# A diffusion-step kernel on one core: lent buffers to the end of their phase, a quiet inverse, and a row normed ahead

## The chip, the cores and the metric

The kernel runs on one core of one Trainium2 chip. The metric is the device time of one execution in microseconds (us), the median over several executions. The engines are called as the profile calls them: PE (TensorE, its matrix multiplications), PEld (its weight loads, which overlap PE), DVE (VectorE), ACT (ScalarE), POOL (GpSimd) and SP (SyncE, which here only issues DMAs). All of them run their own queue in order and wait for each other by semaphores.

## The reference, cut to what matters

One transformer-like layer for 128 context tokens and 128 latent tokens, D = 2048, in float32, weights shared by both:

```
h  = rmsnorm(x, norm1_g) * (1 + scale1) + shift1          # scale, shift, gate: six rows of silu(cond) @ w_mod
(hq, hi, ..., gates) = split(h @ w_in)                    # 17440 columns
o_a = hgrn2(...)          # mixer A, gated linear recurrence, both directions
o_b = chunk_mlp(...)      # mixer B
o_c = rmsnorm(gdn_scan(...), onorm_g) * silu(g_raw)       # mixer C, delta rule with an inverse of I + L
merged = sum(sigmoid(gates_i) * (o_i @ w_br_i))
x = x + gate1 * (merged @ w_out)
x = x + gate2 * (square(relu(h2 @ w_ff1)) @ w_ff2)        # h2 = norm and modulation of x by rows 3 and 4
y = rmsnorm(x, final_g)
```

The outputs are y for both token rows and the final states of mixers A and C for the context. In mixer C the latent row starts from a cached state, the context row from zero.

## The kernel before, in words

**Weights stream past stationary activations.** All 256 tokens stay on chip. Each weight matrix is cut into units of 128 x 1024 floats (512 KB). SP issues one DMA per unit in the order of use. For each unit, ACT rounds it to a high part (`wh`, "CAST wh<-raw") and DVE subtracts to get the low part (`wl`), and PE multiplies three products of high and low parts: 24 matmuls of 256 columns or 12 groups of 512. In the profile `pb` are the banks of these products, `pf` are the banks of all smaller work.

**The start phase.** The first 88 units (`self.lend`) are eight groups of eight units of w_mod for rows 0 and 1 (`in_wmods`, used whole, without a split, by short matmuls "pf<-raw,cst") and, between them, 24 units of w_in (`in_win`, `in_winh`). After each group of eight, a `chain` turns the sums into columns (ACT "COPY m<-pf", PE "pf<-sel,m", DVE "modc", "gs"), and `modulate` makes two columns of the normalised input (DVE "tp", ACT "ACTIVATE tp" and "CAST Hh", DVE "Hl"). The w_in units of a group need the columns of that group.

**Where units land.** There are three load buffers of their own (`raw`). In the start phase, twelve more are lent from six large slots (z3, z4, z5, z6, z7, z0, two halves each) that later hold other things. `run_stream` takes buffers from a list `raws` in first-in order; `issue` loads as long as the list holds one, and a buffer goes back to the list once its unit has been split or used whole. A lent one goes back only while the number of issued units is under `last`; `last = self.lend - len(raws)` is 88 - 15 = 73. Two pairs of high and low parts (slots z8 and z9) are lent in the same way.

**The order of all other work is made by a planner in the program.** `Clock` and `Meter` keep an estimated time for each engine as instructions are written out. Work beside the stream is written as generators (fillers). `pump` lets them go on while DVE and ACT are estimated to be less than a margin ahead of PE. A DMA is estimated to take its bytes divided by 3.6e5 per us, after those before it. Nothing of this estimate runs on the chip: what comes out is one fixed order per engine.

**Modulation sums in the background.** Rows 2 to 5 of w_mod are summed on DVE (`mods`: "junk<-mraw,cb", two sums for each of 128 units `in_wmodr`). `quota(m)` says how many stream units must have gone before unit m of these may be summed: 24 until 30 units after the start phase, 84 until the mark b (which stands ahead of the third branch product `in_wbr`), 96 until 24 units before the end of w_out, the rest in the feed-forward part.

**Mixer C.** `gdn_all` first makes eight blocks and spills them to memory ("sp<-z"), then inverts 32 x 32 diagonal blocks with 31 steps on DVE ("m<-m,m"), then runs `gdn_second` for eight pairs of heads in two chains (slots z3 and z4): four for the latent row (s = 1), then four for the context row. Each reloads a spilled block ("z<-sp"), and those of the latent row also a cached state ("z<-in_s0gd"). Then `norm_gate` norms both rows (`head_rms`), gates them, transposes them and splits them into `och` and `ocl`, which the third branch product needs.

Of the kernel before, what the change touches and what calls it, by code (L numbers as in the profile page):

```python
# [116 lines left out]
class Meter:  # L117
# [34 lines left out]
    def __getattr__(self, name):  # L152
# [3 lines left out]
        def g(*a, **k):  # L156
# [5 lines left out]
            if name == "dma_start":  # L162
# [3 lines left out]
                clock.dma = max(clock.dma, start + DMA0) + size / 3.6e5  # L166
# [30 lines left out]
class Backbone:  # L197
# [173 lines left out]
    def rsqrt(self, v, n, tag, scale=None):  # L371

        nc = self.nc
        r, t = self.small(n, f"rs{tag}"), self.small(n, f"rt{tag}")
# [17 lines left out]
    def run_stream(self, steps):  # L392
# [10 lines left out]
        last = self.lend - len(raws)  # L403
# [366 lines left out]
    def quota(self, m):  # L770

        a, b, c, d, e = self.marks
        for n, lo, hi, n1 in ((0, a, a+30, 24), (24, a+30, b, 84), (84, b, c, 96)):
            if m < n1:
                return lo + (hi - lo) * (m - n) / (n1 - n)
        return d + (e - d) * (m - 96) / 32

    def mods(self, chs):
# [15 lines left out]
        for m, (ch, kq, n) in enumerate(todo):  # L794
# [8 lines left out]
            while not self.forced and self.units < self.quota(m):  # L803
                yield W
# [18 lines left out]
    def head_rms(self, x4):  # L823

        nc = self.nc
        ss = self.small(16, "ss")
        for s in range(2):
            for f in range(2):
                i, t = yield from self.gettmp()
                for h in range(4):  # L830
                    c = 8 * s + 4 * f + h
                    nc.scalar.activation(t[:, h * P:h * P + P], x4[:, s, 4 * f + h, :], AF.Square, accum_out=ss[:, c:c + 1])
# [4 lines left out]
        r = yield from self.rsqrt(ss, 16, "hd")  # L837
        yield W
        for s in range(2):
            for h in range(8):  # L840
                nc.scalar.activation(x4[:, s, h, :], x4[:, s, h, :], AF.Copy, scale=r[:, 8 * s + h:8 * s + h + 1])
                yield 1

    def norm_gate(self, otm, gate, gcol, hi, lo):
# [3 lines left out]
        yield from self.head_rms(otm)  # L848

        def part(j):  # L850
            o = otm[:, :, 2 * j:2 * j + 2, :]
            nc.vector.tensor_tensor(out=o, in0=o, in1=gate[:, :, 256 * j:256 * j + 256].rearrange("p s (h d) -> p s h d", h=2), op=ALU.mult)
# [381 lines left out]
    def gdn_all(self):  # L1234
# [16 lines left out]
        yield 1.2  # L1251
        for j in range(31):
# [5 lines left out]
            yield 0.15 + 2.1e-3 * n * w  # L1258
        nc.vector.transpose(self.AD.rearrange("p m c -> p c m"), X)
# [8 lines left out]

        def chain2(zb):
            for g in range(zb, 8, 2):  # L1270
                yield from self.gdn_second(1 - g // 4, g % 4, zb)

        yield from self.together(chain2(0), chain2(1))
        self.och, self.ocl = self.slot(8, [P, 8, 256], F32R), self.slot(9, [P, 8, 256], F32R)
        yield from self.norm_gate(self.otC, self.gC, self.gdnn, self.och, self.ocl)
# [160 lines left out]
    def run(self):  # L1436
# [3 lines left out]
        self.units = 0  # L1440
# [568 lines left out]
```

## Time and profile before

| | us |
|---|---|
| median of 3 executions | 2002.61 (2000.73 to 2003.5) |
| the profiled execution's own time | 2000.7 |
| its span, first to last instruction | 1998.9 |
| PE busy in the span | 1941.3 (97%) |
| DVE busy | 1407.2 (70%) |
| ACT busy | 952.6 (48%) |
| DMA, mean over the span | 229 GB/s read from memory |
| mean granted PE clock | 0.990 |

The busy time of PE is modelled from pipelined matmuls, so idle PE time is what to look for: stretches in which PE sat still and what ended them. PEclk is the share of full clock that PE was granted. All instructions are written by one helper, so all carry line L173, and groups are told apart by tile names (`out<-in`). Views of stages give busy time per engine in stretches counted from the start of the span.

### The profile page before, as it was taken

The page shows a single profiled execution, that of the slowest core. Times are in us where ns is not written, and L with a number is a line of the kernel's source. Part 1 is how long each engine was busy: PE and PEld are TensorE (multiplying, and loading weights), DVE is VectorE, ACT ScalarE, POOL GpSimd, SP SyncE. Part 2 cuts the span into 40 slices and gives each one's busy share as a digit, 9 for nine tenths or more (in the row PEclk, how much of TensorE's full clock was granted, in tenths as well). Part 3 has the DMA queues.
Part 4 walks back from the last instruction along what each step waited for, and adds up shares of the span by engine and source line. Part 5 has one row for each costly group of instructions (what it writes and reads, how often), then busy time and mean ns, then how long its engine had stood idle before and what let it go on. Part 6 is the DMA issues. An engine that isn't in the chain of part 4 may idle for free.

```text
span 1998.9 us, 30561 instructions
## 1 busy us (share of the span) xinstructions
PE 1941.3 (97%) x11927; PEld 1707.3 (85%) x11927; DVE 1407.2 (70%) x2064; ACT 952.6 (48%) x1419; POOL 49.0 (2%) x120
## 2 busy tenths in 40 slices
PE   6979999999999999999999999899999999999997
PEld 3758988999888889888887888899988998998886
DVE  2325898989887998856876896766766766555476
ACT  3324646476655545366543445544444443344334
POOL 0000000000000001011000000000000000000000
PEclk9999999999999999999999999999999999999999
DMA  9956667565656866756678786566667666566664
GB/s 374 403 205 225 224 209 248 188 231 190 210 186 230 269 221 228 271 176 202 234 237 308 246 282 211 182 220 225 228 225 250 218 235 230 189 203 210 210 233 148
DMA packets 125216, 460.51 MB, mean 230 GB/s; under 512 B 14416, under 2 KB 14992, under 8 KB 122896
## 3 DMA queue, kind: packets, MB, share of 16 engines
q1 hardware_dynamic: 117072, 423.96, 62.6%
q0 software_dynamic: 7568, 34.35, 5.0%
q8 instruction: 93, 1.52, 0.3%
q14 instruction: 51, 0.42, 0.1%
q10 hardware_dynamic: 432, 0.26, 0.0%
HBM read 447.97 MB, written 10.53 MB: 229 GB/s over the span
## 4 chain that ended last, share of the span: by engine, by line
PE 89%; DMA 4%; DVE 3%; ACT 2%; issue 1%; POOL 0%; ACTq 0%; POOLq 0%; DVEq 0%
PE pb L173 80%; PE pf L173 9%; DVE wl L173 1%; DMA raw<-in_win 1%; DVE z L173 1%; ACT wh L173 1%; DMA raw<-in_wff2c 1%; DMA par<-in_par 1%; DMA z<-in_win 1%; DVE m L173 0%; ACT tp L173 0%; DMA z<-in_wmods 0%; ACT z L173 0%; DMA z<-sp 0%; DMA z<-in_s0gd 0%
## 5 line engine op out<-in xcount | busy, mean ns | idle before, releaser
L173 DVE TENSOR_TENSOR wl<-raw,wh 128x1024 fp32r<-128x1024 f32 x586 | 712.3, 1220 | 442.1 <-ACT wh L173 440.5
L173 ACT CAST wh<-raw 128x1024 fp32r<-128x1024 f32 x586 | 612.5, 1048 | 801.3 <-PE pb L173 677.0
L173 PE MATMUL pb<-Hh,wh 128*128 128x256 f32 (+1 forms) x1856 | 529.1, 288 | 9.3 <-ACT wh L173 8.4
L173 PE MATMUL pb<-Hh,wl 128*128 128x256 f32 (+1 forms) x1856 | 525.5, 286 | 4.3 <-DVE wl L173 4.3
L173 PE MATMUL pb<-Hl,wh 128*128 128x256 f32 (+1 forms) x1856 | 510.7, 285 | 0.0
L173 PE MATMUL pb<-wh,z 128*128 128x512 f32 x1368 | 428.2, 392 | 0.0
L173 PEld LDWEIGHTS pb<-Hh,wh 128*128 128x128 f32 (+1 forms) x1856 | 358.8, 193 | 20.5 <-ACT wh L173 11.3
L173 PEld LDWEIGHTS pb<-Hh,wl 128*128 128x128 f32 (+1 forms) x1856 | 359.0, 193 | 6.3 <-DVE wl L173 6.0
L173 PEld LDWEIGHTS pb<-Hl,wh 128*128 128x128 f32 (+1 forms) x1856 | 350.0, 193 | 0.1
L173 PE MATMUL pb<-wh,Hh 128*128 128x512 f32 (+1 forms) x800 | 315.7, 395 | 0.1
L173 DVE SCALAR_TENSOR_TENSOR junk<-mraw,cb 128x1024 bf16<-128x1024 f32 x256 | 312.0, 1219 | 3.1 <-DMA cb<-csd 1.8
L173 PE MATMUL pb<-wl,Hh 128*128 128x512 f32 (+1 forms) x800 | 306.2, 383 | 1.4 <-DVE wl L173 1.4
L173 PE MATMUL pb<-wh,Hl 128*128 128x512 f32 (+1 forms) x800 | 306.2, 383 | 0.0
L173 PEld LDWEIGHTS pb<-wh,z 128*128 128x128 f32 x1368 | 257.6, 188 | 55.7 <-ACT z L173 0.2
L173 PE MATMUL pb<-wl,z 128*128 128x512 f32 x684 | 268.8, 393 | 2.0 <-DVE wl L173 2.0
L173 PEld LDWEIGHTS pb<-wh,Hl 128*128 128x128 f32 x800 | 151.0, 189 | 29.8
L173 PEld LDWEIGHTS pb<-wl,Hh 128*128 128x128 f32 x800 | 151.4, 189 | 28.1 <-DVE wl L173 2.4
L173 PEld LDWEIGHTS pb<-wh,Hh 128*128 128x128 f32 x800 | 151.3, 189 | 27.4 <-ACT wh L173 0.5
L173 PEld LDWEIGHTS pb<-wl,z 128*128 128x128 f32 x684 | 128.4, 188 | 32.2 <-DVE wl L173 4.1
L173 DVE TENSOR_TENSOR z<-z,z 128x512 f32<-128x512 f32 (+4 forms) x101 | 71.7, 743 | 13.3 <-ACT z L173 12.5
L173 DVE SCALAR_TENSOR_TENSOR cy<-z,par,cy 128x258 f32<-128x258 f32 (+1 forms) x192 | 53.6, 331 | 1.9
L173 PEld LDWEIGHTS pf<-m,z 128*128 128x128 f32 x384 | 49.1, 191 | 3.3 <-ACT z L173 0.4
(189 smaller groups left out, 1276.3 us busy)
## 6 DMA issues: line engine op xcount, KB each, us to landing
raw<-in_win SPq DMA_DIRECT2D x246, 512.0 KB, 4.2
raw<-in_wff SPq DMA_DIRECT2D x224, 512.0 KB, 3.8
mraw<-in_wmodr SPq DMA_DIRECT2D x128, 512.0 KB, 4.8
raw<-in_wbr SPq DMA_DIRECT2D x48, 512.0 KB, 3.8
z<-in_wmods SPq DMA_DIRECT2D x44, 512.0 KB, 10.0
raw<-in_wmods SPq DMA_DIRECT2D x20, 512.0 KB, 7.9
cb<-csd POOLq DMA_DIRECT2D x8, 1024.0 KB, 7.7
raw<-in_wouta SPq DMA_DIRECT2D x16, 512.0 KB, 4.4
```

The lines of the kernel that those rows point to most:

```text
L173: return f(*a, **k)
```

## The change

Six edits.

1. `last = self.lend`: a lent load buffer goes back to the list until all 88 units of the start phase have been issued.
2. The planner estimates a DMA by 4.05e5 bytes per us in place of 3.6e5.
3. While the 31 steps of the inverse are written out, a flag `quiet` keeps `mods` from starting another unit.
4. `quota` allows 90 units in place of 84 until the mark b.
5. `head_rms` and `norm_gate` can do one token row alone. A new generator `latent_row` waits until each chain of mixer C has done two pairs (all of the latent row), then norms and gates that row (`gated_row`); `norm_gate` afterwards norms and gates the context row and transposes both. Norming one row means 8 in place of 16 columns in the small operations, done twice.
6. The small tiles of `rsqrt` are allotted with 16 columns always.

```diff
-                clock.dma = max(clock.dma, start + DMA0) + size / 3.6e5
+                clock.dma = max(clock.dma, start + DMA0) + size / 4.05e5
...
-        r, t = self.small(n, f"rs{tag}"), self.small(n, f"rt{tag}")
+        r, t = (self.small(16, f"{x}{tag}")[:, :n] for x in ("rs", "rt"))
...
         raws = [0, 1, 2] + [t[:, h, :] for t in lent for h in range(2)]
-        last = self.lend - len(raws)
+        last = self.lend
...
-        for n, lo, hi, n1 in ((0, a, a+30, 24), (24, a+30, b, 84), (84, b, c, 96)):
+        for n, lo, hi, n1 in ((0, a, a+30, 24), (24, a+30, b, 90), (90, b, c, 96)):
...
-            while not self.forced and self.units < self.quota(m):
+            while not self.forced and (self.quiet or self.units < self.quota(m)):
                 yield W
...
-    def head_rms(self, x4):
+    def head_rms(self, x4, rows=(0, 1)):
...
-        for s in range(2):
+        for a, s in enumerate(rows):
             for f in range(2):
...
-    def norm_gate(self, otm, gate, gcol, hi, lo):
+    def gated_row(self, otm, gate, s):
+
+        yield from self.head_rms(otm, (s,))
+        for c in (0, 512):
+            o = otm[:, s].rearrange("p h d -> p (h d)")[:, c:c + 512]
+            self.nc.vector.tensor_tensor(out=o, in0=o, in1=gate[:, s, c:c + 512], op=ALU.mult)
+            yield 0.0
+
+    def norm_gate(self, otm, gate, gcol, hi, lo, done=()):
...
-        yield from self.head_rms(otm)
+        rows = [s for s in range(2) if s not in done]
+        yield from self.head_rms(otm, rows)
...
-            o = otm[:, :, 2 * j:2 * j + 2, :]
+            o = otm[:, rows[0]:rows[-1] + 1, 2 * j:2 * j + 2, :]
...
+        self.quiet = True
         for j in range(31):
...
+        self.quiet = False
...
+        latents = [0, 0]
+
         def chain2(zb):
             for g in range(zb, 8, 2):
                 yield from self.gdn_second(1 - g // 4, g % 4, zb)
+                latents[zb] += 1
+
+        def latent_row():
+            while min(latents) < 2:
+                yield W
+            yield from self.gated_row(self.otC, self.gC, 1)
 
-        yield from self.together(chain2(0), chain2(1))
+        yield from self.together(latent_row(), chain2(0), chain2(1))
...
-        yield from self.norm_gate(self.otC, self.gC, self.gdnn, self.och, self.ocl)
+        yield from self.norm_gate(self.otC, self.gC, self.gdnn, self.och, self.ocl, done=(1,))
```

What this makes of the engines' queues, at three places.

The first is SP's queue near the end of the start phase, from the 73rd unit on (the first row here). `raw_..` are the three own buffers, `z0` to `z7` lent ones; `mraw` are units of the background sums. Before:

```order
L173 DMA z0_16_138<-in_win 128x1024
L173 DMA raw_82_800<-in_wmods 128x1024
L173 DMA raw_83_804<-in_wmods 128x1024
L173 DMA raw_90_859<-in_wmods 128x1024
L173 DMA mraw_95_891<-in_wmodr 128x1024
L173 DMA mraw_96_893<-in_wmodr 128x1024
L173 DMA raw_104_989<-in_winh 128x1024
L173 DMA raw_105_993<-in_wmods 128x1024
L173 DMA raw_106_997<-in_wmods 128x1024
L173 DMA raw_109_1004<-in_wmods 128x1024
L173 DMA raw_110_1032<-in_win 128x1024
```

Now, from the same unit:

```order
L173 DMA z0_16_138<-in_win 128x1024
L173 DMA z0_16_138<-in_wmods 128x1024
L173 DMA z6_14_136<-in_wmods 128x1024
L173 DMA raw_82_802<-in_wmods 128x1024
L173 DMA raw_83_806<-in_winh 128x1024
L173 DMA z4_12_134<-in_wmods 128x1024
L173 DMA z3_11_133<-in_wmods 128x1024
L173 DMA mraw_90_861<-in_wmodr 128x1024
L173 DMA mraw_91_863<-in_wmodr 128x1024
L173 DMA raw_96_875<-in_wmods 128x1024
L173 DMA z4_12_134<-in_win 128x1024
L173 DMA z6_14_136<-in_wmods 128x1024
```

The order of the units is the same; of the last fifteen, which all went through the three own buffers, three still do (raw_82, raw_83, raw_96), and twelve go through lent ones.

The second is ACT's queue in the last two groups of the start phase: the casts of the w_in units (into `wh` or into the lent pairs z8 and z9), the copy of the last group's sums ("COPY m1"), and the modulation after it ("ACTIVATE tp", "CAST Hh"). Before:

```order
L173 CAST wh_107_1000<-raw_104_989 128x1024
L173 CAST z8_113_1042<-raw_110_1032 128x1024
L173 CAST z9_115_1071<-raw_114_1045 128x1024
L173 COPY m1_119_1084<-pf_103_986 96x512
L173 ACTIVATE tp_120_1104<-tp_120_1104,modc_89,gs_90 128x128 x4
L173 CAST Hh_26_191<-tp_120_1104 128x512
L173 CAST wh_121_1123<-raw_116_1074 128x1024
L173 CAST wh_124_1129<-raw_117_1078 128x1024
```

Now:

```order
L173 CAST z8_108_1013<-z4_12_134 128x1024
L173 CAST z9_109_1045<-z5_13_135 128x1024
L173 CAST wh_111_1052<-z0_16_138 128x1024
L173 CAST wh_113_1080<-z3_11_133 128x1024
L173 CAST wh_115_1086<-z7_15_137 128x1024
L173 COPY m1_117_1092<-pf_106_999 96x512
L173 ACTIVATE tp_118_1118<-tp_118_1118,modc_89,gs_90 128x128 x4
L173 CAST Hh_26_194<-tp_118_1118 128x512
L173 CAST wh_119_1156<-z7_15_137 128x1024
```

Three casts (wh_111, wh_113, wh_115) that stood behind the last group's modulation now stand ahead of it.

The third is POOL's queue in the second half of mixer C, where it reloads the spilled blocks of the context row (`sp0` to `sp3`), clears parts of them, stores the final states (`out_stgd`) and loads the small weights of mixer B (`in_wsT`). Before:

```order
L173 DMA cb_1077_7935<-csd_853 128x2048
L173 DMA z4_1087_7983<-sp1_5979 128x1024
L173 DMA z3_1094_8020<-sp0_5978 128x1024
L173 MEMSET z4_1087_7983 32x4x32 x4
L173 MEMSET z3_1094_8020 32x4x32 x4
L173 DMA out_stgd<-tp_1129_8207 256x1x256
L173 DMA z4_1130_8210<-sp3_5981 128x1024
L173 MEMSET z4_1130_8210 32x4x32 x4
L173 DMA tp_1151_8352<-in_wsT 128x256
```

Now:

```order
L173 DMA cb_1048_7810<-csd_851 128x2048
L173 DMA z4_1058_7859<-sp1_5912 128x1024
L173 MEMSET z4_1058_7859 32x4x32 x4
L173 DMA z3_1077_7959<-sp0_5911 128x1024
L173 MEMSET z3_1077_7959 32x4x32 x4
L173 DMA out_stgd<-tp_1103_8123 256x1x256
L173 DMA z4_1104_8126<-sp3_5914 128x1024
L173 MEMSET z4_1104_8126 32x4x32 x4
L173 DMA out_stgd<-tp_1126_8259 256x1x256
L173 DMA z3_1127_8262<-sp2_5913 128x1024
L173 MEMSET z3_1127_8262 32x4x32 x4
```

The two chains now alternate, and the last pair (`sp2`) is reloaded ahead of mixer B's weights, where before it came after them.

More of the change, by code (lines that the diff above doesn't have):

```diff
@@ L820, in mods @@
                 self.moddone.add(ch)
-    def head_rms(self, x4):
+    def head_rms(self, x4, rows=(0, 1)):
         nc = self.nc
-        ss = self.small(16, "ss")
-        for s in range(2):
+        n = 8 * len(rows)
+        ss = self.small(16, "ss")[:, :n]
+        for a, s in enumerate(rows):
             for f in range(2):
@@ L830, in head_rms @@
                 for h in range(4):
-                    c = 8 * s + 4 * f + h
+                    c = 8 * a + 4 * f + h
                     nc.scalar.activation(t[:, h * P:h * P + P], x4[:, s, 4 * f + h, :], AF.Square, accum_out=ss[:, c:c + 1])
@@ L836, in head_rms @@
         nc.vector.tensor_scalar(out=ss, in0=ss, scalar1=1.0 / P, scalar2=EPS, op0=ALU.mult, op1=ALU.add)
-        r = yield from self.rsqrt(ss, 16, "hd")
+        r = yield from self.rsqrt(ss, n, "hd")
         yield W
-        for s in range(2):
+        for a, s in enumerate(rows):
             for h in range(8):
-                nc.scalar.activation(x4[:, s, h, :], x4[:, s, h, :], AF.Copy, scale=r[:, 8 * s + h:8 * s + h + 1])
+                nc.scalar.activation(x4[:, s, h, :], x4[:, s, h, :], AF.Copy, scale=r[:, 8 * a + h:8 * a + h + 1])
                 yield 1
-    def norm_gate(self, otm, gate, gcol, hi, lo):
+    def gated_row(self, otm, gate, s):
[5 more added lines that the diff above has]
+    def norm_gate(self, otm, gate, gcol, hi, lo, done=()):
         nc = self.nc
-        yield from self.head_rms(otm)
+        rows = [s for s in range(2) if s not in done]
+        yield from self.head_rms(otm, rows)
         def part(j):
-            o = otm[:, :, 2 * j:2 * j + 2, :]
-            nc.vector.tensor_tensor(out=o, in0=o, in1=gate[:, :, 256 * j:256 * j + 256].rearrange("p s (h d) -> p s h d", h=2), op=ALU.mult)
+            o = otm[:, rows[0]:rows[-1] + 1, 2 * j:2 * j + 2, :]
+            g = gate[:, rows[0]:rows[-1] + 1, 256 * j:256 * j + 256].rearrange("p s (h d) -> p s h d", h=2)
+            nc.vector.tensor_tensor(out=o, in0=o, in1=g, op=ALU.mult)
             yield W
@@ L1439, in run @@
         self.rowgen, self.rowd = {}, {}
-        self.units = 0
+        self.units, self.quiet = 0, False
         self.setup()
```

## The prediction

> **What bounds the kernel now.** I read the stretches by stage first, for idle PE time, then what PE waited for in the worst stretch, then the queues that end those waits.
>
> ```profile
> 0.00:100.00 100.00, 80.98 (x515) 51.43 (x516) 29.02 (x48) 36.20 (x58) 1.95 (x7) 0.97 1.00 389
> 100.00:175.00 75.00, 60.94 (x404) 46.74 (x403) 22.13 (x33) 24.84 (x37) 1.07 (x2) 0.91 0.57 198
> 175.00:700.00 525.00, 524.79 (x3411) 476.94 (x3410) 456.62 (x805) 296.15 (x502) 11.63 (x30) 0.99 0.66 221
> 700.00:1110.00 410.00, 403.39 (x2233) 348.37 (x2232) 308.28 (x461) 205.14 (x356) 27.46 (x68) 1.00 0.70 235
> 1110.00:1300.00 190.00, 183.58 (x1053) 161.41 (x1052) 149.07 (x222) 89.97 (x129) 2.15 (x4) 0.98 0.67 229
> 1300.00:1950.00 650.00, 650.00 (x4161) 592.58 (x4160) 412.61 (x453) 280.83 (x308) 4.77 (x9) 1.00 0.67 221
> 1950.00:1999.00 49.00, 37.66 (x163) 29.87 (x161) 29.47 (x46) 19.43 (x31) 0.00 (x0) 0.92 0.43 148
> ```
>
> The columns are the stretch, its length, busy time of PE, PEld, DVE, ACT and POOL with counts, PEclk, DMA share and GB/s. PE is the bound: from 175 to 700 us it idles 0.2 us, from 1300 to 1950 nothing. The work of PE is not changed, so the change can win only idle PE time and time at a lowered clock. It idles 19 us before 100 and 11 us after 1950, which the change does not touch, 6.6 us from 700 to 1110, 6.4 us from 1110 to 1300, and 14.1 us between 100 and 175, with the clock down to 0.91. There the DMA engines, full until 100 (share 1.00, 389 GB/s), are only 57% busy.
>
> ```profile
> PE pb L173 <- ACT wh L173: 6.1, 2, 3.9
> PE pb L173 <- ACT z L173: 4.7, 2, 3.8
> PE pb L173 <- DVE z L173: 1.8, 2, 0.9
> PE pb L173 <- DVE wl L173: 1.6, 2, 0.9
> 102.18 0.33 SPq L173 DMA_DIRECT2D z<-in_win  x1
> 106.25 7.06 SPq L173 DMA_DIRECT2D raw<-in_wmods  x3
> 129.86 0.33 SPq L173 DMA_DIRECT2D raw<-in_winh  x1
> 161.69 0.33 SPq L173 DMA_DIRECT2D raw<-in_winh  x1
> 133.50 1.04 ACT L173 CAST wh<-raw 128x1024 fp32r<-128x1024 f32 x1 [2.73 <-DMA raw<-in_winh]
> 134.59 0.58 PE L173 MATMUL pb<-Hh,wh 128*128 128x256 f32 x1 [3.91 <-ACT wh L173]
> 146.75 0.39 PE L173 MATMUL pb<-Hh,z 128*128 128x256 f32 x1 [3.76 <-ACT z L173]
> 118.00:130.00 12.00, 12.00 (x87) 7.91 (x88) 2.86 (x8) 2.94 (x6) 0.56 (x1) 1.00 0.28 104
> ```
>
> The first four rows are PE's waits from 112 to 162: total, times, longest. They sum to 14.2 us in four stops. The rest show why. The 73rd unit is issued at 102.18; from there lent buffers no longer come back, and the next units go through three. The unit of 129.86 had to wait until PE had used its predecessor; it landed at 133.5, the cast followed at once, and PE, which had nothing else, started at 134.59. The stop at 146.75 is the same thing again, and the last of the 88 units was issued at 161.69. Meanwhile, from 118 to 130, the DMA engines carried 104 GB/s. So PE waits for loads that were issued late for want of a buffer, while bandwidth lay idle.
>
> **The change, part by part.** *Lent buffers to the end.* The two late loads end stops of 3.91 + 0.68 and 3.76 + 0.88 us (the second figure is the wait for the low part). SP's new queue keeps the order of the units but takes buffers freed long before: of the last fifteen units, the first six need only what PE and DVE have released by about 112, and the last of them (in z7) what PE releases at about 124. Fifteen units of 0.524 MB, two of the background and its 1 MB row of coefficients are 10 MB; at 389 GB/s that is 26 us from 102.2 on, so all land by about 130. With its stop taken off, PE needs the unit of 134.59 at about 130, and the last one six units of 2.9 us and two groups of sums later, at about 149, so these loads are covered.
>
> *The cast order.* The two other stops are short: 0.92 + 0.88 us at 114 and 2.17 + 0.88 at 160.5. There the data lay ready but the cast stood in ACT's queue behind a modulation.
>
> ```profile
> 152.42 1.90 PE L173 MATMUL pf<-raw,cst 128*32 128x512 f32 x8
> 154.36 0.58 ACT L173 COPY m<-pf 96x512 f32<-96x512 f32 x1 [1.87 <-PE pf L173]
> 157.16 1.65 ACT L173 ACTIVATE tp<-tp,modc,gs 128x128 f32<-128x128 f32 x4 [2.21 <-DVE tp L173]
> 156.58 0.28 PE L173 MATMUL pb<-Hl,z 128*128 128x256 f32 x1
> 156.94 0.28 PE L173 MATMUL pb<-Hl,z 128*128 128x256 f32 x1
> 158.84 0.62 ACT L173 CAST Hh<-tp 128x512 fp32r<-128x512 f32 x1
> 160.46 0.38 PE L173 MATMUL pb<-Hh,wh 128*128 128x256 f32 x1 [2.17 <-ACT wh L173]
> ```
>
> In the new order of ACT three casts stand ahead of the last copy, so the unit of 160.46 has its high part before the modulation begins. What is late next is the first unit that needs the modulated columns. From the end of the last sums (154.3) to the low part of the columns takes 154.36 to 159.46 plus a subtraction of 0.68, about 6 us; two units of 24 matmuls cover it with 5.8 us (three matmuls from 156.58 to 156.94 make 0.12 each) and the short "sel" between them. That leaves 0 to 1 us there. The first modulation leaves up to 0.5 us in the same way. If the casts turn out to be late by their own chain (1.04 for a cast, 1.23 for a subtraction, 2.3 us for each of three stops), 6.9 us stay. I take 2.5 us as what remains, nearer to the lower end (0.5), since ACT was busy 24.8 of 75 us here.
>
> *The clock.* After each longer stop PE runs slow for a while.
>
> ```profile
> 136.00:142.00 6.00, 6.00 (x32) 5.15 (x35) 0.00 (x0) 0.00 (x0) 0.00 (x0) 0.57 0.30 100
> 148.00:154.00 6.00, 5.99 (x31) 4.65 (x31) 1.23 (x1) 1.05 (x1) 0.00 (x0) 0.72 0.27 90
> 160.00:166.00 6.00, 4.67 (x24) 4.47 (x25) 4.09 (x4) 2.92 (x4) 0.00 (x0) 0.72 0.50 150
> 590.00:600.00 10.00, 10.00 (x43) 8.59 (x43) 7.51 (x15) 3.44 (x6) 0.00 (x0) 0.66 0.52 181
> ```
>
> Busy time times the missing clock is 6.0 x 0.43 + 6.0 x 0.28 + 4.7 x 0.28 = 5.6 us. Matmuls were not back to back all through, so I take 5.0. Without the stops this goes too.
>
> The Trainium skill's page "TensorE: Matmul & The Clock Gate", section "Part 1: The HAM clock gate (the "warmup" mystery)", says the clock falls to half only after an idle window of about 3.4 us. By that rule only the first two stops cost clock, the third dip would have another cause and stay, and the gain would be 1.3 us smaller. The trace agrees for the first two, but the dip after 160 follows 2.17 + 0.88 us, and at 590 the clock fell with PE never idle, so I count all three.
>
> *The planner's faster DMA.* It moves rows, and costs nothing by itself. Up to about 100 us the queues are the same but for a few rows of PE near 18 us, where PE waits for the first w_in unit anyway.
>
> *No sums under the inverse.* This removes nothing:
>
> ```profile
> 722.00:769.00 47.00, 0.00 (x0) 0.00 (x0) 1.00 0.64 204
> 769.00:1110.00 341.00, 82.18 (x134) 0.00 (x0) 1.00 0.70 239
> 769.00:1110.00 341.00, 244.10 (x338) 1.00 0.70 239
> 1110.00:1250.00 140.00, 109.98 (x140) 1.00 0.71 245
> L173 DVE SCALAR_TENSOR_TENSOR junk<-mraw,cb 128x1024 bf16<-128x1024 f32 x256 | 312.0, 1219 | 3.1 <-DMA cb<-csd 1.8
> L173 DVE DVE_READ_ACCUMULATOR junk<-mraw,cb 128x1 f32 x256 | 21.0, 82 | 0.0
> ```
>
> The first two rows are the sums alone (`junk`), the next two all of DVE. In the inverse (722 to 769) there is not one sum before either; gain 0. *The quota* moves 6 units, 12 sums of 1.30 us (1.22 and the read of the accumulator) or 15.6 us, into 769 to 1110, where DVE has 97 us free, out of 1110 to 1250, where it has 30. *The latent row* repeats five small operations and moves the rest; no row of it is waited for:
>
> ```profile
> 975.76 1.41 DVE L173 SCALAR_TENSOR_TENSOR z<-pf,par,z 128x512 fp32r<-128x512 f32 x2
> 1115.96 0.39 PE L173 MATMUL pb<-wh,z 128*128 128x512 f32 x1
> 862.36 0.63 PE L173 MATMUL pf<-ident,z 128*128 128x128 f32 x4 [2.19 <-DMA z<-sp]
> DMA to landing us min/median/max: 3.8/5.7/7.3
> ```
>
> Mixer C's result is split at 977 and first used at 1116, a cover of 139 us. Its ending earlier is worth nothing; if it ended 139 us later it would cost. What PE does wait for in mixer C is a reload, 2.19 us at 862, with 3.8 to 7.3 us to land. PE's order had 12 stream matmuls between the last use of that buffer and the first of the next block; now no reload has fewer than 15, which went without a wait. But two reloads of the latent row have fewer than before. I put this, the sums and the re-planned order together at 0, between a gain of 4 (most of the 6.6 and 6.4 us is not theirs) and a loss of 4.
>
> **The sum.** 14.2 + 5.0 - 2.5 + 0 = 16.7 us. The profiled execution took 2000.7, so 1984.0; it is the lowest of the executions shown, and from the median of 2002.6 it is **1985.9, said as 1986**.
>
> **The rivals.** *Forecast*, 0.60: 1982 to 1990.5 (remainders 0.5 to 5, the middle 4 either way).
>
> *The stops shrink to the cast chain*, 0.21: 6.9 us remain and the middle gives back 2, so 14.2 + 5.0 - 6.9 - 2 = 10.3 and 1992. For it: five casts and a copy in a row on ACT, with three buffers for high parts. Against: ACT idle two thirds of the time.
>
> *More than that*, 0.08: no remainder, all 5.6 of the clock and 3 from the middle, 22.8, so 1980.
>
> *Given back later*, 0.07: the stretch after it is bound by DVE, not PE (457 of 525 us busy), and the 17 us come back as waits for `wl`: 2002. Against: sums are rationed by units, not by time, and PE idled 0.2 us there.
>
> *Slower*, 0.04: a deep queue of loads does not keep the rate. The fifteen units are 7.9 MB; before, the last was issued at 161.69 and there at about 165. Below 7.9 MB / 63 us = 125 GB/s they would land later than that; at the 104 GB/s of 118 to 130 the last lands at 178, 13 us late: 2015. Against: 389 GB/s with the same deep queue up to 100.
>
> **Range and chances.** 1980 to 1996 holds the first three cases and the tail of the second, all but about 2 in 10. A measurement here can tell about 0.2%, 4 us, from no change. Faster by more: 0.60 + 0.21 + 0.08 = 0.89, and 0.01 of the fourth; no change 0.06; slower 0.04.
>
> **What would show it.** Right: PE idle between 100 and 155 at most 3 us, PEclk near 1.00 there, the fifteen units issued by 125 without a pause, and the first unit after the start phase reached 15 to 18 us earlier. The unchanged counts of `junk` in the inverse, and no wait for "z<-sp" over 1 us. Wrong: stops of over 2 us at the units cast after the copies, a clock that dips all the same, or waits for `wl` between 175 and 700.

## The result and the profile after

The changed kernel takes 1981.66 us (median of 4 executions, 1976.65 to 1983.67); the kernel before, measured beside it, 2001.67 (4 executions, 2000.09 to 2003.5). The ratio is 0.9898, with a 95% interval of 0.9879 to 0.9917: about 20 us, or 1%, faster. 1986 was predicted, with a range of 1980 to 1996. The profiled execution took 1980.8 us, its span is 1979.0 (before 2000.7 and 1998.9).

First the view by stretches of the changed kernel, with the columns of the prediction's first view (stretch, length, busy time of PE, PEld, DVE, ACT and POOL with counts, PEclk, DMA share, GB/s):

```profile
0.00:100.00 100.00, 79.84 (x522) 50.31 (x525) 29.87 (x49) 36.29 (x58) 1.96 (x7) 0.98 1.00 391
100.00:175.00 75.00, 75.00 (x582) 62.67 (x574) 38.25 (x54) 34.36 (x48) 1.07 (x2) 1.00 0.72 269
175.00:700.00 525.00, 522.14 (x3327) 470.67 (x3326) 465.95 (x839) 298.66 (x511) 13.79 (x34) 1.00 0.66 222
700.00:1110.00 410.00, 402.16 (x2221) 348.09 (x2220) 310.49 (x451) 202.31 (x347) 25.29 (x64) 1.00 0.71 240
1110.00:1300.00 190.00, 184.10 (x1138) 165.59 (x1137) 136.20 (x199) 92.02 (x134) 2.14 (x4) 0.98 0.63 207
1300.00:1950.00 650.00, 650.00 (x4081) 589.10 (x4080) 416.02 (x456) 280.37 (x308) 4.76 (x9) 1.00 0.68 223
```

Between 100 and 175 us PE is busy for all 75.00 us, at full clock; before it was busy 60.94 us at 0.91. The stretches behind it look much as they did: PE idles 2.9 us from 175 to 700 (before 0.2), 7.8 from 700 to 1110 (6.6), 5.9 from 1110 to 1300 (6.4). SP's queue shows how the start phase was mended. The timeline of SP in the changed kernel (start, time, engine, operation):

```profile
105.41 0.33 SPq L173 DMA_DIRECT2D raw<-in_wmods  x1
106.25 0.33 SPq L173 DMA_DIRECT2D raw<-in_winh  x1
109.07 2.56 SPq L173 DMA_DIRECT2D z<-in_wmods  x2
...
119.52 1.93 SPq L173 DMA_DIRECT2D z<-in_win  x2
121.96 0.33 SPq L173 DMA_DIRECT2D z<-in_winh  x1
124.78 3.32 SPq L173 DMA_DIRECT2D raw<-in_win  x2
```

and two stretches of it:

```profile
118.00:130.00 12.00, 12.00 (x89) 8.82 (x88) 4.19 (x6) 5.83 (x10) 0.00 (x0) 1.00 1.03 415
130.00:142.00 12.00, 12.00 (x89) 8.82 (x88) 6.25 (x9) 4.25 (x7) 0.00 (x0) 1.00 0.43 166
```

The last of the 88 units is issued at 121.96 (before at 161.69), and from 118 to 130 the DMA engines move 415 GB/s, where they moved 104 before. At 124.78 the stream behind the start phase begins to load.

To see where the time went, the matmuls of the stream can be counted: all kernels here issue the same 10320 of them (`pb`), so the start of the same one can be compared. The table is worked out from the two traces; the 577th is the first behind the start phase.

```
matmul of the stream     289    409    433    457    505    577   1201   6001   10319
before, us             102.1  134.6  146.8  154.3  166.0  174.6  262.8 1299.9  1988.3
after, us              101.3  127.7  132.6  137.5  144.2  152.8  241.1 1279.5  1968.4
gained by then           0.8    6.9   14.2   16.8   21.8   21.8   21.8   20.4    19.9
```

So 21.0 us are gained between the 289th and the 577th matmul, where the four stops were. 1.4 us are given back between there and the 6001st, 0.6 at the end. The 0.8 us before the 289th are none of the change's doing that I can show: the kernels below differ there by -0.4 to 3.2 us from the kernel before, and in the order of the dips of the clock that their traces show before 60 us. Those with two dips of 3.41 us at half clock, as in the kernel before, gain -0.4 to -0.1 us, those with one (the change among them) 0.3 to 1.7, those with none 2.4 to 3.2.

The 21.0 us are 14.1 us of idle PE time (the stops of the prediction) and 6.9 us of clock. The clock can be read exactly when the stretches are cut where it changes, which I had not done. The kernel before:

```profile
134.30:141.13 6.83, 5.86 (x27) 5.34 (x30) 1.23 (x1) 0.24 (x1) 0.00 (x0) 0.50 0.45 163
147.96:151.37 3.41, 3.36 (x15) 3.36 (x16) 0.00 (x0) 0.00 (x0) 0.00 (x0) 0.50 0.49 161
161.61:165.02 3.41, 3.31 (x15) 3.31 (x16) 2.92 (x4) 0.69 (x1) 0.00 (x0) 0.50 0.65 178
```

The clock is halved for 6.83, 3.41 and 3.41 us, 13.65 us in all. PE was busy for 12.5 us of them (5.86, 3.36 and 3.31), which at half clock costs 6.3 us: most of the 6.9 that the count leaves beside the idle time. The other 0.6 us I can't place.

In mixer C the changed kernel has a wait that the kernel before did not have. PE's waits between 540 and 1000 us, the first four (total, times, longest):

```profile
PE pf L173 <- DMA z<-in_s0gd: 3.7, 3, 2.9
PE pb L173 <- DVE wl L173: 2.1, 5, 1.2
PE pf L173 <- DVE wl L173: 1.3, 1, 1.3
PE pf L173 <- DMA z<-sp: 1.2, 2, 0.9
```

The first is 2.87 us at 745.59, for the cached state of the first pair; the 2.19 us for `sp` at 862 are gone, but a smaller wait of the kind is left. The third row, 1.33 us at 817.63, is put down to `wl`; yet the matmuls that wait there transpose a reloaded block (`pf<-ident,z`), and by the trace its load landed at 817.50. In "sums free" below, which has the same instructions, the profile names the reload for that wait (1.09 us at 814.66, the longest of this row):

```profile
PE pf L173 <- DMA z<-sp: 2.1, 2, 1.1
```

The clock changes places in the same way: the dip near 590 is gone, and one of half that length follows the new wait. Stretches of the changed kernel:

```profile
590.00:600.00 10.00, 10.00 (x52) 8.21 (x52) 8.65 (x12) 4.22 (x5) 0.00 (x0) 1.00 0.81 226
745.11:748.52 3.41, 2.93 (x14) 2.96 (x15) 2.06 (x5) 0.81 (x1) 0.00 (x0) 0.50 1.03 417
```

From 175 to 1300 us PE idles 3.4 us more than before (16.6 against 13.2) and has 3.4 us less of half clock, which is worth 1.7 at most: about the 1.4 given back.

### The profile page after: what moved, and what is told of

The parts are those of the page before. It is cut to its first block, busy times and chain, and to the rows that moved or that the text cites. A ratio compares the mean times of both kernels' runs of the same rounds, so it can differ in the third digit from the quotient of the medians.

```text
span 1979.0 us, 30568 instructions
## 1 busy us (share of the span) xinstructions
PE 1930.8 (98%) x11927; PEld 1699.4 (86%) x11927; DVE 1409.8 (71%) x2071; ACT 952.3 (48%) x1420; POOL 49.0 (2%) x120
## 4 chain that ended last, share of the span: by engine, by line
PE 83%; DVE 6%; DMA 5%; issue 3%; ACT 2%; POOL 0%; ACTq 0%; DVEq 0%; POOLq 0%
PE pb L173 76%; PE pf L173 8%; DVE wl L173 2%; DVE z L173 2%; DMA raw<-in_wbr 1%; ACT wh L173 1%; DMA z<-in_s0gd 1%; DVE m L173 1%; DVE junk L173 1%; DMA raw<-in_win 1%; DMA par<-in_par 1%; DMA z<-in_win 1%; DMA z<-in_wmods 0%; ACT z L173 0%; DMA raw<-in_wff2c 0%
## 5 line engine op out<-in xcount | busy, mean ns | idle before, releaser
L173 PE MATMUL pb<-Hh,wh 128*128 128x256 f32 x1872 | 531.6, 286 | 3.7 <-ACT wh L173 2.3
L173 PE MATMUL pb<-Hh,wl 128*128 128x256 f32 x1872 | 527.2, 284 | 2.0 <-DVE wl L173 2.0
L173 PE MATMUL pb<-Hl,wh 128*128 128x256 f32 x1872 | 512.9, 283 | 0.0
L173 PEld LDWEIGHTS pb<-Hh,wh 128*128 128x128 f32 x1872 | 359.6, 192 | 14.8 <-issue 5.0
L173 PEld LDWEIGHTS pb<-Hh,wl 128*128 128x128 f32 x1872 | 359.7, 192 | 3.1 <-DVE wl L173 2.8
L173 PEld LDWEIGHTS pb<-Hl,wh 128*128 128x128 f32 x1872 | 350.8, 192 | 0.1
```

The source lines that it names most:

```text
L173: return f(*a, **k)
```

## The experiments

All ratios are to the kernel before, with 95% intervals, the change's from 4 executions of each, the others' from 4 to 12. The table gives each kernel's result and three readings of its profiled execution: the time gained between the 289th and the 577th matmul of the stream (the start phase), between the 577th and the 6001st (the middle), and PE's idle time from 700 to 1110 us.

```
kernel                        median   ratio  [interval]          start  middle  idle 700-1110
the change                    1981.7   0.9898 [0.9879, 0.9917]    21.0    -1.4     7.8
lent buffers alone            1985.5   0.9921 [0.9903, 0.9939]    15.9    +0.2     6.8
rate alone                    2007.7   1.0046 [1.0033, 1.0060]     2.4    -9.0    11.6
lent buffers and rate         1988.1   0.9942 [0.9928, 0.9955]    21.0   -10.2    11.5
all but lent buffers          1999.8   0.9995 [0.9983, 1.0006]     2.8    +1.1     6.9
all but the rate              1982.9   0.9895 [0.9874, 0.9916]    14.4    +2.3     4.7
all but the quota             1990.2   0.9943 [0.9925, 0.9961]    21.0   -10.5    12.6
all but the latent row        1983.8   0.9910 [0.9891, 0.9929]    21.0    -5.2     9.4
sums free (the same rows)     1980.0   0.9903 [0.9883, 0.9923]    21.0    -0.3     6.4
lent but the last four        1979.4   0.9901 [0.9884, 0.9919]    21.0    +2.0     5.3
lent but the last eight       1986.8   0.9941 [0.9927, 0.9955]    14.0    -0.5     7.7
first reload early            1979.1   0.9891 [0.9872, 0.9910]    21.0    -0.4     7.8
quota even to 96              1978.8   0.9899 [0.9885, 0.9912]    21.0    -4.7     9.7
```

The start column repeats to 0.1 us wherever no stop is left. The middle column scatters: the change and "sums free" are the same instructions and differ by 1.1 us in it. It is also read from one execution, while the executions of one kernel differ by up to 8.0 us ("lent but the last four", 1975.9 to 1983.9, of which the profiled one is the fastest; that of "all but the rate" is the slowest of its six). So differences of a few us in this column decide nothing.

### The lent buffers alone, and everything but them

The kernel before with one edit, and the change without it:

```diff
-        last = self.lend - len(raws)
+        last = self.lend
```

> The kernel before with only the first edit: lent buffers are used to the end of the phase. Theory A (the whole gain is the start phase: idle PE time and the clock that goes with it): PE idle from 100 to 175 us falls from 14 us to under 1, PEclk is 1.00 there, the last of the 88 units is issued by 125, and the time is 1980 to 1983, as with the whole change (1981.7). Theory B (the planner's faster DMA is needed as well, because it orders the loads and casts of the start phase): one or two stops of 1 to 4 us remain between 100 and 175, and the time is 1986 to 1994. If the time is under 1979, the other edits cost something, since the middle of the program is here nearly that of the kernel before.

> The whole change without its first edit: lent buffers are given back 15 units before the end, as before. Theory A: the stops of the start phase are back (10 to 14 us idle between 100 and 175, PEclk about 0.91), the time is 2000 to 2004. Theory B (the other edits carry part of the gain, by the order in which the planner puts loads and casts): 1990 to 1997.

Alone, the edit gives 15.9 of the 21.0 us. Two pairs of short stops remain. The timeline of PE in this kernel, the rows with a wait from 100 to 175 us (the idle time before and its cause in brackets):

```profile
113.60 0.38 PE L173 MATMUL pb<-Hh,z 128*128 128x256 f32 x1 [0.92 <-ACT z L173]
114.86 0.39 PE L173 MATMUL pb<-Hh,z 128*128 128x256 f32 x1 [0.88 <-DVE z L173]
148.28 0.38 PE L173 MATMUL pb<-Hh,wl 128*128 128x256 f32 x1 [0.88 <-DVE wl L173]
150.01 0.39 PE L173 MATMUL pb<-Hl,wh 128*128 128x256 f32 x1 [1.36 <-DVE Hl L173]
```

The first pair is that of the kernel before: a cast stands behind a modulation. The second is what the prediction had named as late next, `Hl` of the modulation and a `wl`. So theory B holds, with a time just under its 1986: for the whole gain of the start phase the planner's rate is needed as well. The two long stops of 3.91 and 3.76 us are this edit's alone: without it they are back (3.66 and 3.81 us, with a third pair of 2.16 and 0.88; 12.1 us idle in all), and the whole gain is gone, as theory A had it (1999.8, just under its 2000).

### How many buffers have to stay

The changed kernel with `last = self.lend - 8`, and with `last = self.lend - 4` (15 before the change).

> The changed kernel, with the lent buffers given back 8 units before the end of the phase instead of at its end (15 before the change). Theory A (each unit that has to go through three buffers at the end may cost a stop of up to 4 us): one long stop near 145 of 3 to 4 us is back, and with it a dip of PEclk to 0.6 to 0.7 over some 6 us (about 2 us), so 1985 to 1988. Theory D (only the first of the late units was critical, since the units behind it are covered by PE's own work): no stop over 1 us, 1980 to 1983.

> The changed kernel, with the lent buffers given back 4 units before the end; PE's order of instructions is that of the changed kernel, and only ten rows of the load queue and of the casts name another buffer. Theory A: the last units through three buffers are covered by the units still ahead of them, no stop over 1 us between 100 and 155, 1980 to 1983. Theory D': the very last load waits as before (its buffer comes free when PE has used its predecessor), one stop of 2 to 4 us near 150, 1983 to 1987.

Four units from the end the buffers cost nothing. Eight from the end they cost 7.0 us in the start phase, but by no long stop: theory A had the time and not the way. PE's waits in that stretch, from the timeline:

```profile
137.42 0.38 PE L173 MATMUL pb<-Hh,z 128*128 128x256 f32 x1 [0.72 <-ACT z L173]
138.68 0.38 PE L173 MATMUL pb<-Hh,z 128*128 128x256 f32 x1 [0.88 <-DVE z L173]
144.72 0.39 PE L173 MATMUL pb<-Hh,wh 128*128 128x256 f32 x1 [0.65 <-ACT wh L173]
145.98 0.38 PE L173 MATMUL pb<-Hh,wl 128*128 128x256 f32 x1 [0.88 <-DVE wl L173]
```

They sum to 3.1 us. The stretches, cut at the clock's steps, show the rest:

```profile
137.10:140.52 3.42, 2.22 (x17) 2.03 (x18) 1.32 (x2) 0.75 (x2) 0.00 (x0) 1.00 0.26 57
140.52:143.93 3.41, 3.41 (x18) 3.26 (x16) 0.84 (x3) 2.47 (x6) 0.00 (x0) 0.50 0.97 387
143.93:147.35 3.42, 1.89 (x13) 1.56 (x13) 2.65 (x3) 2.63 (x3) 0.00 (x0) 1.00 0.21 41
147.35:150.76 3.41, 3.41 (x18) 3.41 (x18) 1.45 (x2) 1.05 (x1) 0.00 (x0) 0.50 0.89 296
```

Twice, 3.41 us at half clock follow a stretch of the same length in which PE was busy for 2.22 and 1.89 us. 18 matmuls go through in such a stretch, where the kernel with the lent buffers alone has 31 from 152.13 to 155.54, and of the 7.0 us lost in the start phase 3.9 are left beside the stops. Two such stretches at half clock account for 3.4 of them, so the clock cost about as much as the stops ahead of it.

### The rate, the quota and the latent row

With the first two edits alone I expected the whole gain.

> The kernel before with the first two edits alone: lent buffers to the end, and the planner's rate of 4.05e5 bytes per us. Sums, quota and the order of mixer C's norm are those of before. With the first edit alone the time was 1985.5, two pairs of short stops behind the modulations being left (0.92 + 0.88 at 113.6, 0.88 + 1.36 at 148.3); in the whole change the planner puts the casts ahead of those modulations. Theory A (the two edits are the whole gain, since the rate alone moves the casts): no PE stop over 0.2 us between 100 and 175, the first unit after the start phase as early as with the whole change, 1979 to 1983. Theory B (the other edits carry part of the last 4 us): 1984 to 1987.

The start phase is mended, as theory A had it, and 10.2 us are lost again behind it: 1988.1, above theory B's 1987. So theory B holds in that some other edit carries time, but for more than its 4 us, and not in the start phase. Two runs take one of them out each, a third takes out the rate:

```diff
 # all but the latent row
-        yield from self.together(latent_row(), chain2(0), chain2(1))
+        yield from self.together(chain2(0), chain2(1))
 # all but the quota
-        ... (24, a+30, b, 90), (90, b, c, 96)
+        ... (24, a+30, b, 84), (84, b, c, 96)
 # all but the rate, and (from the kernel before) its reverse, the rate alone
-                clock.dma = max(clock.dma, start + DMA0) + size / 4.05e5
+                clock.dma = max(clock.dma, start + DMA0) + size / 3.6e5
```

> The changed kernel without its last edit: mixer C's latent row is normed and gated together with the other row, as before. Lent buffers, rate, quota and the pause of the sums stay. The kernel with the first two edits alone took 1988.1, 8 us of its gain given back behind 800 us: a PE stop of 4.07 us at 922.7, where the stream reaches products of another mixer (pb<-wh,z) that are ready late, and 6.8 us of half clock behind it. Theory E (the latent row, taken out of the work at the end of mixer C, is what lets that other mixer's chain finish in time): the stop of about 4 us before the first pb<-wh,z is back, 1986 to 1990. Theory F (the quota is): no such stop, 1979 to 1983.

> The changed kernel with the old quota of 84 units for the modulation sums; lent buffers, rate and the latent row ahead stay. Theory F (the six units of sums that the quota moves are what keeps DVE free for the chain in front of the first pb<-wh,z, or orders it in time): the stop of about 4 us near 920 is back, 1986 to 1990. Theory E (the latent row): no such stop, 1979 to 1983. If neither this run nor the one without the latent row has the stop, either edit alone is enough to move the planner's order; if both have it, both are needed.

> The changed kernel with the planner's old rate of 3.6e5; the four other edits stay. Theory A' (the rate's part is the cast order of the start phase alone): the two pairs of short stops are back, 0.92 + 0.88 near 114 and about 0.9 + 1.4 near 148, the first unit after the start phase comes 5 to 6 us later than with the whole change, and the time is 1985 to 1988, as with the first edit alone. Theory G (the middle is re-planned as well, so that its order decides): below 1983 or above 1990.

> The kernel before with only the planner's rate of 4.05e5. Theory H (with the old quota the new rate re-plans the middle so that the four spatial parts in front of the stream's products near 920 come late, whatever the start phase does): PE idle falls by about 2 us between 100 and 120 and grows by 4 to 7 us near 935, with a dip of the clock there; about 2 us of the start phase won, some 9 lost behind 770 us, so 2004 to 2008, slower than before. Theory I (the loss came from the stream running ahead of the mixers, which only the lent buffers bring about): no such stop, 1997 to 2000.

It is the quota (theory F). With the old one the loss is back, 1990.2, just over the 1990 given. What happens there is told by the timeline of the kernel with all but the quota, POOL's load of mixer B's small weights and PE's rows:

```profile
912.73 0.54 POOL L173 DMA_DIRECT2D tp<-in_wsT  x1 [8.32 <-issue]
917.31 2.00 PE L173 MATMUL pf<-tp,z 128*128 128x128 f32 x8 [2.81 <-DMA tp<-in_wsT]
923.22 0.79 PE L173 MATMUL pb<-wh,z 128*128 128x512 f32 x1 [3.91 <-ACT z L173]
```

against the same places of the whole change:

```profile
893.76 0.54 POOL L173 DMA_DIRECT2D tp<-in_wsT  x1 [0.35 <-issue]
...
918.79 0.39 PE L173 MATMUL pb<-wh,z 128*128 128x512 f32 x1
```

The stream comes to the products of mixer B (`pb<-wh,z`) at about 919 us, and mixer B has four small weights to load and four parts to compute first. In the change the last of these loads is issued 25.0 us ahead of the first product and nothing waits. With the old quota it comes 10.5 us ahead, and PE waits 6.7 us in two stops. Against the change, this kernel loses 9.1 us between the 577th and the 6001st matmul: 4.4 are idle PE time, and 10.24 us at half clock from 917.36 on, in which PE was busy for 6.33, cost 3.2; 1.5 us I can't place. With the rate alone it is the same:

```profile
923.39 0.54 POOL L173 DMA_DIRECT2D tp<-in_wsT  x1 [1.78 <-PE pb L173]
935.30 1.16 PE L173 MATMUL pf<-tp,z 128*128 128x128 f32 x8 [0.63 <-DVE z L173]
940.53 0.79 PE L173 MATMUL pb<-wh,z 128*128 128x512 f32 x1 [4.07 <-ACT z L173]
```

17.1 us ahead, a stop of 4.07, and from 937.58 to 944.40 half the clock. The rate alone makes the kernel slower, 1.0046 [1.0033, 1.0060], as theory H had it: the stream need not run early for this. In every kernel that was run with the new rate and the old quota (three of them) the last load comes 10.5 to 17.1 us ahead, and PE stops for 3.9 to 4.1 us at the first product. In the kernel before (903.2 and 936.6) and in all the others, with the old rate or the new quota, the lead is 25 to 35 us and there is no such stop. The lead of the load is only a sign of it, since with the rate alone the last load is not what PE waits for. The cause stands in PE's own queue. Counted in the traces, the three kernels with the stop have no matmul of the stream between the last part (`pf<-tp,z`) and the first product (the two PE rows shown of each are neighbours in the timeline); the eleven others have 51 to 108 there (the change 69, the kernel before 84). So the steps behind the last part, up to ACT's write of the `z` that the product needs, have nothing to cover them, and PE waits for them, 3.9 to 4.1 us. The planner writes mixer B's parts that late with the new rate and the old quota; which of its comparisons turns on the quota I did not trace, and that stays open. More sums on DVE in that stretch are not the cause: from 840 to 925 us the kernel with the old quota has 18 rows of `junk`, the change 22.

The latent row's edit is worth little: without it there is no stop of this kind (theory F, with a time just over its 1983), the profiled execution loses 5.2 us in the middle (3.8 more than the change's: 1.6 more of idle time from 700 to 1110 in small waits, and 3.41 us more at half clock behind the wait at 744), and the ratio of 0.9910 [0.9891, 0.9929] overlaps the change's. Whether it gives 2 us or none these runs can't tell.

Without the new rate, but with the rest, the kernel is as fast as the change (0.9895 [0.9874, 0.9916]); the stops are back, as theory A' said, and the first unit after the start phase comes 7.8 us later than in the change, not 5 to 6; but the time is below 1983, if barely, as theory G had it. The middle is 3.7 us better than in the change's profiled execution. So the rate gives 5 to 7 us at the start by its order of casts (21.0 against 15.9 and 14.4), costs 9 to 10 in the middle with the old quota, 0 to 4 with the new, and comes to nothing that these runs can tell in the sum.

### The quota by degrees

```diff
-        for n, lo, hi, n1 in ((0, a, a+30, 24), (24, a+30, b, 90), (90, b, c, 96)):
+        for n, lo, hi, n1 in ((0, a, a+30, 24), (24, a+30, b, 96)):
```

> The changed kernel with the quota spread evenly over all 96 sums up to the second mark (90 of them there in the change, 84 before). Theory J (the sums' pace matters by degrees: the earlier they run, the less DVE has to do behind 1100 us and the earlier the spatial parts come): no stop near 920, waits in the 700 to 1300 us stretch as with 90 or up to 2 us less, 1979 to 1982. Theory K (it matters by which order the planner happens to find): anything from a stop of 3 to 5 us somewhere between 770 and 1110 to none, 1979 to 1990, not in order of the quota.

No stop near 919 (the last load is issued at 890.5, the first product comes at 919.1), and the time is that of the change. DVE is busy 126 us from 1110 to 1300, where it was 136, which helps nobody: PE idles 5.9 us there in both. But two waits in mixer C, 1.38 us at 789.01 and 2.06 at 818.04, are larger than in the change (0.62 and 1.33). The profile puts them down to `junk` and `wl`, but the reloads that the waiting matmuls read landed 0.1 us before each ended. Theory J is right on the stop and the time, and not on the waits, which are 1.9 us more from 700 to 1110; theory K allows all of this. A reading by degrees is not shown by three values, of which two are alike.

### The same instructions twice, and the first reload issued early

The change without `self.quiet = True` gives the same instructions in the same order on every engine. So the third edit does nothing here, and the run shows how far two builds of one program lie apart.

> The changed kernel with the modulation sums allowed under the inverse again. The program's rows come out the same on every engine as with the whole change, so both theories expect 1981.7 within 0.1%; what it differs by is how far two builds of one program lie apart.

It took 1979.96 us, 1.7 less than the change beside another set of runs, at the same ratio within the intervals.

The other kernel takes the new wait at 745.59 away: the first pair of each chain is reloaded, with its state, ahead of the inverse.

```diff
+        self.early = {}
+        for hp in range(2):
+            z = self.early[hp] = self.slot(3 + hp, [P, 2048])
+            nc.gpsimd.dma_start(z[:, 0:1024], self.spill[4 + hp])
+            nc.gpsimd.dma_start(z[:, 1024:1536].rearrange(...), self.I["s0gd"][:, :, 2 * hp:2 * hp + 2, :])
+        yield W
         self.quiet = True
         for j in range(31):
```

> The changed kernel, with the two first reloads of mixer C's second half (the spilled block and the state) issued ahead of the 31 steps of the inverse instead of behind it; they have some 45 us to land, where PE waited 2.87 us for the state at 745.6 us of the changed kernel. Theory A (every stop of PE in mixer C counts in full): that wait goes, 1978 to 1980. Theory C (the wait hides another one, the next step of the chain has to wait for the same reason, for an eviction or a sum): the wait goes, another of 1 to 3 us stands in its place, 1981 to 1983.

The stop of 2.87 us goes. Its place is taken by smaller ones: the longest in mixer C is 0.90 us, again for a state, and eight waits for `wl` make 3.3 us. PE's idle time from 700 to 1110 is 7.8 us in both. The median is the second lowest of all, 1979.05, and lies in theory A's range; but its interval [0.9872, 0.9910] overlaps those of the change and of its twin, and the idle time is unchanged, as theory C had it, though in waits smaller than its 1 to 3 us. So the times don't decide between the two; by the trace the wait was not worth its length. None of these kernels beats the change by more than the intervals.

## Why the prediction came out as it did

**What bounds the kernel: right.** The gain is the idle PE time between 100 and 175 us and the clock that went with it, and nothing else: 21.0 us there, against 19.9 over the whole span. The first unit after the start phase comes 21.8 us earlier, more than the 15 to 18 given as a sign, because nothing was left of the stops and the clock was worth more.

**The lent buffers: right, and the cover held.** All units were issued by 121.96, as expected by 125, at 415 GB/s, and PE had no wait in the stretch. The two long stops belong to this edit alone.

**The cast order: right in what it does, wrong in whose it is.** The prediction read the three casts ahead of the last copy in the order of the whole change and put them with the lent buffers. They take the planner's rate as well: with the lent buffers alone one of the three stands there, with the rate alone none, with both all three. With the lent buffers alone the two pairs of short stops cost 4.0 us.

**"It moves rows, and costs nothing by itself" is the first step that failed.** I looked for the rate's effect in the first 100 us, and took the moved rows behind it for the other edits'. Alone it makes the kernel slower by 0.46%; in the start phase, beside the lent buffers, it is worth 5 to 7 us.

**The remaining stops were put at 2.5 us and are 0.** The stop that I had for late next (`Hl`) exists in the kernel with the lent buffers alone, 1.36 us behind 0.88 for `wl`. In the change the casts and subtractions of the next units are done before the modulation begins. Without the rate 4.0 us remain: within the 0.5 to 5 given, above the 2.5 chosen.

**The clock was put at 5.0 us and gave 6.9.** The term was mis-sized by the way it was read: stretches of 6 us laid over dips that begin at 134.30, 147.96 and 161.61 left out the first 1.70 us of the first and mixed the third with time in which PE stood still, which gave 5.6; then 0.6 more was taken off. Cut at its steps, the same trace gives 13.65 us at 0.50, or 6.3 us by PE's busy time in them.

The Trainium skill, "TensorE: Matmul & The Clock Gate", section "Part 1: The HAM clock gate (the "warmup" mystery)", would by its idle window have left the third dip; the trace went against it, since that dip went with its stop. The same section's statement that the window is free-running and 3413 ns long does agree with the trace: the dips last 3.41 or 6.83 us and begin whole multiples of that apart (134.30, 147.96 and 161.61).

**The middle was put at 0, and "the quota moves 6 units" was costed as DVE time only: the second step that failed.** The sum came out near 0, -1.4 us in the profiled execution, but by luck, as the difference of two terms of about 9 us which the prediction did not have: the rate's loss at mixer B, and the quota, which takes that loss away. The argument that the sums had room on DVE was true, and did not bear on it. With a planner, the cost of an edit is not that of the work it moves; what had to be compared were the places in the order, the first product of mixer B above all.

**The reloads were half right.** The 2.19 us for `sp` went, but a wait of over 1 us for a reload is left by the reading above (1.33 at 817.63), where the prediction allowed none, and one of 2.87 us for the state is new. By my count of stream matmuls no reload had grown tight. But the new wait came at the first pair, which is reloaded at the end of the inverse, and there a count from the last use of the buffer says nothing; what counts is when the load is issued and how long it takes. Both come out worse for PE with the planner's new rate: in the ten kernels that have it and issue this load behind the inverse, PE is ready for the first use 5.2 us after the issue and the state lands after 7.6 to 8.3 us, beyond the 7.3 that the prediction had as the longest, so PE waits 2.6 to 3.3 us. In the three with the old rate it is 5.5 to 5.6 and 5.4 to 6.7 us, and PE waits 0 to 1.3. Why these loads take longer I did not trace; at 745 us of the change the DMA engines were fully busy (share 1.03, 417 GB/s).

**The sums under the inverse: right.** The flag changes no instruction. The sixth edit, and the quota without the new rate and the rest, were not run by themselves.

**The rivals.** "The stops shrink to the cast chain" is the kernel with the lent buffers alone, 1985.5, with 4.0 us of stops where I had 6.9. The measured 1981.66 lies just under the forecast's own 1982 to 1990.5. That interval is narrower than its terms, since 0.5 to 5 us remaining and 4 either way give 1980 to 1992. "More than that" came nearest in its parts: no remainder, the whole of the clock (more than its 5.6), but a small loss in the middle where it had a gain. "Given back later" had the right sort of mechanism at the wrong place: not waits for `wl` between 175 and 700 (1.8 us in all there), but mixer B at 919, and only with the old quota. The deep queue kept its rate.

In the sum, 16.7 us were predicted and 19.9 measured in the span: +2.5 for the remainder, +1.9 for the clock (0.6 of it not placed), +0.8 from before 100 us, -1.4 for the middle, -0.6 at the end.

## What to carry to other kernels

Where a program plans its own order, an edit of an estimate or a quota is no small edit: here two of them were worth some 9 us each with opposite signs, and the sum hid both. Take such edits apart one by one, and look at the first place where the stream needs each side computation: how much of the stream stands in PE's queue between the last step of that computation and this place (51 matmuls or more without a wait, none with a stop of 4 us) told more here than how busy the engine was that seemed to be the bottleneck. And read the clock by its own steps: a stop costs its length and often, behind it, whole stretches at half clock.

## What the runs showed of the hardware

The steps of PE's clock lie on a fixed grid of 3.41 us within an execution, and where the grid lies differs from one to the next. Whether a stop costs clock can depend on where it falls in the grid. The kernel with the lent buffers alone and the one with all but the rate have the same second pair of stops (0.88 and 1.36 us, 0.88 and 1.35). The first:

```profile
145.30:148.71 3.41, 2.48 (x17) 1.88 (x15) 1.71 (x2) 3.38 (x5) 0.00 (x0) 1.00 0.00 0
148.71:152.13 3.42, 2.12 (x17) 2.12 (x18) 2.38 (x3) 0.15 (x1) 0.00 (x0) 1.00 0.02 5
```

The second:

```profile
148.50:151.91 3.41, 1.64 (x11) 1.44 (x12) 3.24 (x4) 1.00 (x2) 0.00 (x0) 1.00 0.02 5
151.91:155.32 3.41, 3.41 (x18) 3.41 (x17) 0.00 (x0) 0.56 (x1) 0.00 (x0) 0.50 0.00 0
```

In the first the grid cut the pair of stops in two, PE was busy 2.48 and 2.12 us of the two stretches, and the clock stayed. In the second one stretch held most of it, 1.64 us busy, and 3.41 us at half clock followed. The start phase is 1.5 us longer there (14.4 against 15.9 gained). But busy time alone doesn't decide: 2.22 us was followed by a dip with the last eight buffers given back, 2.12 was not here, and neither was 1.72 us in the same kernel later (845.04 to 848.45). And in the kernel before the clock was at 0.50 from 591.69 to 598.52 behind a stretch in which PE was busy throughout:

```profile
588.28:591.69 3.41, 3.41 (x29) 3.28 (x28) 3.38 (x6) 1.06 (x4) 0.00 (x0) 1.00 0.63 175
```

The prediction took this dip as evidence against an idle rule. A dip like it, 3.4 to 6.8 us long, stands between 575 and 599 us in the five kernels that lack the new rate or the lent buffers wholly (the one before among them), and in none of the nine that have both. What the busy time hides is the size of the matmuls. PE's timeline there, in the kernel before:

```profile
588.95 0.95 PE L173 MATMUL pf<-ones,tp 128*128 128x1 f32 x8
589.75 1.04 PE L173 MATMUL pf<-gG,tri 128*128 128x16 f32 x8
590.65 1.03 PE L173 MATMUL pf<-ones,tp 128*128 128x1 f32 x8
```

Of the 27 matmuls that begin in this stretch 24 have at most 16 columns, and together the 27 have 1648. Cutting all fourteen traces at their clock's grid from 60 to 1950 us, the stretches in which PE was busy for over 3.3 us and the clock fell right behind are these five, with 1648 to 2159 columns (22 to 24 of the short matmuls). No other busy stretch at full clock has fewer than 2666; the same short matmuls run in the nine other kernels too, but there no stretch of the grid from 500 to 660 us holds more than 18 of them. So a stretch full of very short matmuls goes with a dip in these traces, busy or not. No kernel was run to test it, and the count of columns alone doesn't decide where PE also idles: the stretch with 1.72 us busy had 2048 columns. The rule stays open.
